# One decoder layer on one core: the first norm's outputs spread over more steps, its last squares added on VectorE, the last norm's scaled identity in one operation

## The chip, the core and the metric

The kernel runs on one core of one Trainium2 chip. The metric is the time on the device in microseconds (us), median of several runs. The engines are TensorE (PE in the profile: matrix products), VectorE (DVE), ScalarE (ACT), GpSimd (POOL) and SyncE (SP, which here only issues DMAs). Each works through its own queue of instructions in order and waits on semaphores for the others.

## What is computed

One layer of a hybrid decoder, 1024 tokens by 2048 channels, float32. What touches the change is the end of it, the output projection and the layer norm:

```python
def layer_norm(x, gain, bias):
    xf = x.astype(jnp.float32)
    mu = jnp.mean(xf, axis=-1, keepdims=True)
    var = jnp.mean(jnp.square(xf - mu), axis=-1, keepdims=True)
    y = (xf - mu) * lax.rsqrt(var + LN_EPS)
    return (y * gain.astype(jnp.float32) + bias.astype(jnp.float32)).astype(x.dtype)
...
    a = banded_sink_attention(q, k, v, sinks, bias_hqk, valid) * jax.nn.silu(g_attn)
    b = multiscale_pool(u_pool, w_pool, pool_scale) * jax.nn.silu(g_pool)
    mix = jnp.einsum('bsc,cd->bsd', jnp.concatenate([a, b], axis=-1), w_out)
    ple = jax.nn.sigmoid(jnp.einsum('bsd,de->bse', x, w_gate_ple)) * jnp.einsum('bsp,pd->bsd', p_i, w_ple)
    return layer_norm(DEEPNORM_ALPHA * x + mix + ple, ln_gain, ln_bias)
```

## The kernel before

Everything is held transposed: a tile has 128 channels on the partitions and tokens along the free dimension. The 2048 channels are 16 blocks (`NB`). Every product of a weight block with an operand is three matmuls (`mm3`, lines 181 to 183), since each float32 is split into a rounded part and a rest (`wh`, `wl` for weights, names ending in `h` and `l` for operands). The split of a weight tile `raw` is made in `make_unit`: a copy on ScalarE into `wh` (line 232) and a subtraction on VectorE into `wl` (`lo`, recorded at line 124, the helper `tt` of all two-input operations). `wh` and `wl` have four buffers each, `raw` has five of two halves, so the splits run up to four half-products ahead of TensorE. `raw` tiles are loaded on SP's queue.

The output projection runs over the last phases in two parts: the first 768 tokens (`F1`) by a seven-product scheme, and the last 256 (`F2`) plainly in `run_plain`, 16 blocks of two half-products. A half-product here is 12 matmuls of 256 columns, and every second one adds a 13th that subtracts the mean (`less_mean`, line 823). Its results lie in the PSUM banks `qa` and `qb`, two buffers each; VectorE adds each into a tile (`t1h`, `t1l`, `t2h` are parts of larger buffers that hold the 16 blocks), which is called its evacuation below. ScalarE then squares the block (line 833, into `t2l` or `t2h`), and VectorE adds the squares up.

The norm of the first 768 tokens (`one`) is finished during the plain phase of the last 256. `norm_square` has added up the squares of 15 blocks in the tile `sq`; those of the 16th stay in a tile `q` of their own. `norm_scale` sums both over the channels by matmuls with a column of ones (line 842, into `pv`), VectorE makes the variance from it (line 860), POOL raises it to the power -1/2 (`st`, through line 124), ScalarE multiplies the identity by it, block by block of 128 tokens (line 865, `dg`: six operations for 768 tokens), and a matmul with ones spreads the result over all partitions (`norm_spread`, line 849, the "spread"), which ScalarE copies back into `sq` (line 850). Then `norm_out` does, for each of the 16 blocks, a multiply on VectorE (`d` or `part` <- `sq`, 128x768), a scaling with gain and bias on ScalarE (line 127), and two DMAs to the output, on POOL's queue for the first 14 blocks and on SP's for the last two.

The norm of the last 256 tokens (`two`) comes after the last half-product and goes the same way, with two operations at line 865; its spread (line 871) stays in PSUM, and `norm_out_two` treats the blocks in pairs.

What sets the order: the kernel counts steps. One step (`tick`) is one half-product in the plain phase, 32 in all. `later(n, fn)` writes `fn` into the program n steps on. A list scheduler may then shift instructions of one engine past one another, which it did at a few places of TensorE's order.

Of the kernel before, what the change touches and what calls it, by code (L numbers as in the profile page):

```python
# [26 lines left out]
AF = mybir.ActivationFunctionType  # L27
ALU = mybir.AluOpType
# [3 lines left out]
P = 128  # L32
# [31 lines left out]
class Layer:  # L64
# [100 lines left out]
    def later(self, n, fn):  # L165

        def run():
            with ExitStack() as ctx:
                for ins in self.latest.values():
                    ctx.enter_context(self.tc.issue_after(ins))  # L170
                fn()
        self.after(n, run)
# [656 lines left out]
    def norm_square(self, L, j, d, wait=1):  # L829
        L["d"][j] = d  # L830
        last = len(L["d"]) == NB
        q = L["new"]("sq" if not L["parts"] else "q")
        self.nc.scalar.activation(q, d, AF.Square)
        if last or not L["parts"]:
            L["parts"].append(q)
        else:
            self.later(wait, lambda: self.tt(L["parts"][0], L["parts"][0], q, ALU.add))
# [14 lines left out]
    def norm_scale(self, L, wait=0):  # L852

        nc, n = self.nc, L["n"] // P
        st = self.tile(self.sm, [P, 64], "st")
        var, rstd = st[:, :n], st[:, 32 : 32 + n]
        sums = self.bank("pv", 1, (P, 16))
        for i, a in enumerate(L["parts"]):
            self.norm_sums(sums, a, i == 0, i == len(L["parts"]) - 1)
        nc.vector.tensor_scalar(out=var, in0=sums[:, :n], scalar1=1.0 / D, scalar2=EPS, op0=ALU.mult, op1=ALU.add)  # L860
        self.tt(rstd, var, self.mhalf[:, :n], ALU.pow, nc.gpsimd)
        dg = L["new"]("dg")
        for b in range(n):
            f = slice(b * P, b * P + P)
            nc.scalar.activation(dg[:, f], self.ident, AF.Copy, scale=rstd[:, b : b + 1])
        if wait:
            L["a"] = L["parts"][0]
            self.later(wait, lambda: self.norm_spread(L, L["a"], self.ones, dg))
        else:
            L["a"] = self.bank("sc", 2)[:, : L["n"]]  # L870
            nc.tensor.matmul(L["a"], self.ones, dg[:, : L["n"]], start=True, stop=True)
# [24 lines left out]
    def run(self):  # L896
        nc, tc, fix = self.nc, self.tc, self.fix
# [94 lines left out]
        parts, work, over = ExitStack(), ExitStack(), ExitStack()  # L992
# [75 lines left out]
        t = 9  # L1068
# [109 lines left out]
        for k in range(4):  # L1178
# [4 lines left out]
        one = self.one = self.norm_begin(F1, 0, lambda kind: self.tile(lns, [P, F1], "sq" if kind == "sq" else "q", F32R if kind == "hi" else F32,  # L1183
                                                                       bufs=1 if kind == "sq" else 2))
# [13 lines left out]
        for k in range(4):  # L1198
            r = rest_x[k]
            f = slice((k % 2) * 2 * F2, (k % 2) * 2 * F2 + 2 * F2)  # L1200
# [28 lines left out]

        two = self.norm_begin(F2, F1, new)  # L1230
        self.second_done = lambda b, c: self.norm_square(two, b, c)
        self.later(3, lambda: self.norm_scale(one, 1))
        for j in range(NB):
            self.later(5 + 12 * j // 16, lambda j=j: self.norm_out(one, j))
        for i in range(8):
            self.run_plain(g + i)
        self.drain()
# [58 lines left out]
```

## Time and profile before

| | |
|---|---|
| median of 3 runs | 1483.82 us |
| lowest and highest | 1481.38 and 1485.56 us |
| span of the profiled execution, first to last instruction | 1484.2 us |
| mean granted TensorE clock | 0.992 |
| plain phase, first matmul to the second norm's sums | 1412.20 to 1468.90 us |
| second norm and its outputs | 1468.90 to 1484.2 us |

The span is the only time that the profiled execution has here; nothing around it is recorded. It lies 0.4 us over the median and within the runs. Times in the profile's rows count from the start of the span. A row of the timeline shows start, length, engine, line, operation, out<-in, shape and count; in square brackets stands the idle time of the engine before it and what ended it. Lengths are from issue to completion, so the next instruction on the engine can begin before the last one's length is over.

### The profile page before, as it was taken

The page shows a single profiled execution, that of the slowest core. Times are in us where ns is not written, and L with a number is a line of the kernel's source. Part 1 is how long each engine was busy: PE and PEld are TensorE (multiplying, and loading weights), DVE is VectorE, ACT ScalarE, POOL GpSimd, SP SyncE. Part 2 cuts the span into 40 slices and gives each one's busy share as a digit, 9 for nine tenths or more (in the row PEclk, how much of TensorE's full clock was granted, in tenths as well). Part 3 has the DMA queues.
Part 4 walks back from the last instruction along what each step waited for, and adds up shares of the span by engine and source line. Part 5 has one row for each costly group of instructions (what it writes and reads, how often), then busy time and mean ns, then how long its engine had stood idle before and what let it go on. Part 6 is the DMA issues. An engine that isn't in the chain of part 4 may idle for free. (4 is left out here: it accounts for less than half of the span.)

```text
span 1484.2 us, 20552 instructions
## 1 busy us (share of the span) xinstructions
PE 1448.0 (98%) x6972; PEld 1223.3 (82%) x6972; DVE 1119.9 (75%) x2027; ACT 778.7 (52%) x1548; POOL 286.5 (19%) x404
## 2 busy tenths in 40 slices
PE   9999999999999999999999999999999999999996
PEld 6788888888887888888887778888887888899986
DVE  7788578888797877889667957675678566987785
ACT  5464566655666555666534443333256333554484
POOL 0000123332322333231111111110011111111231
PEclk9999999999999999999999999999999999999998
DMA  7563975445445555457847577987598768585464
GB/s 265 208 217 100 255 212 178 142 163 181 168 170 178 169 185 178 166 194 249 199 140 203 147 246 213 278 250 210 144 336 260 199 185 226 138 245 128 149 228 163
DMA packets 106106, 291.93 MB, mean 197 GB/s; under 512 B 12112, under 2 KB 17616, under 8 KB 106000
## 3 DMA queue, kind: packets, MB, share of 16 engines
q1 hardware_dynamic: 81936, 212.21, 42.3%
q0 software_dynamic: 20736, 71.05, 20.2%
q10 hardware_dynamic: 3328, 7.34, 1.5%
q8 instruction: 55, 0.90, 0.2%
q14 instruction: 51, 0.42, 0.1%
HBM read 200.38 MB, written 90.18 MB: 196 GB/s over the span
## 5 line engine op out<-in xcount | busy, mean ns | idle before, releaser
L232 ACT CAST wh<-raw 128x512 fp32r<-128x512 f32 x428 | 264.1, 619 | 446.0 <-PE qa L182 146.4
L124 DVE TENSOR_TENSOR wl<-raw,wh 128x512 fp32r<-128x512 f32 x428 | 299.8, 704 | 118.9 <-ACT wh L232 115.8
L402 ACT COPY part<-qa 128x512 f32<-128x512 f32 (+1 forms) x180 | 103.7, 576 | 49.7 <-PE qa L183 49.1
L607 POOL TENSOR_SCALAR_AFFINE_SELECT s<-s 128x512 fp32r<-128x512 f32 x128 | 100.6, 798 | 140.6 <-ACT s L600 99.0
L124 DVE TENSOR_TENSOR part<-part,qb 128x512 f32<-128x512 f32 (+1 forms) x120 | 80.9, 674 | 50.4 <-PE qb L183 47.7
L181 PE MATMUL qa<-b11h,wh 128*128 128x512 f32 (+2 forms) x292 | 111.1, 381 | 2.1 <-ACT b11h L258 1.4
L182 PE MATMUL qa<-b11l,wh 128*128 128x512 f32 (+2 forms) x292 | 110.0, 377 | 0.2 <-DVE b11l L124 0.2
L183 PE MATMUL qa<-b11h,wl 128*128 128x512 f32 (+2 forms) x292 | 110.0, 378 | 0.0
L181 PE MATMUL qb<-b21h,wh 128*128 128x512 f32 (+2 forms) x292 | 109.5, 375 | 0.0
L182 PE MATMUL qb<-b21l,wh 128*128 128x512 f32 (+2 forms) x292 | 108.7, 372 | 0.0
L183 PE MATMUL qb<-b21h,wl 128*128 128x512 f32 (+2 forms) x292 | 108.6, 372 | 0.0
L181 PE MATMUL qa<-t2h,wh 128*128 128x512 f32 (+1 forms) x260 | 101.5, 390 | 5.4 <-ACT part L402 3.3
L181 PE MATMUL qb<-t1h,wh 128*128 128x512 f32 (+1 forms) x260 | 100.9, 388 | 3.4 <-DVE part L124 1.4
L183 PE MATMUL qa<-t2h,wl 128*128 128x512 f32 (+1 forms) x260 | 100.8, 388 | 3.1 <-DVE wl L124 3.1
L181 PE MATMUL qa<-t3h,wh 128*128 128x512 f32 (+1 forms) x260 | 100.9, 388 | 0.2 <-ACT part L402 0.2
L181 PE MATMUL qa<-t4h,wh 128*128 128x512 f32 (+1 forms) x260 | 100.4, 386 | 0.3 <-DVE part L124 0.3
L181 PE MATMUL qb<-b22h,wh 128*128 128x512 f32 (+1 forms) x260 | 100.3, 386 | 0.0
L182 PE MATMUL qa<-t2l,wh 128*128 128x512 f32 (+1 forms) x260 | 100.1, 386 | 0.0
L182 PE MATMUL qa<-t3l,wh 128*128 128x512 f32 (+1 forms) x260 | 99.8, 384 | 0.0
L183 PE MATMUL qb<-t1h,wl 128*128 128x512 f32 (+1 forms) x260 | 99.7, 384 | 0.0
L182 PE MATMUL qb<-t1l,wh 128*128 128x512 f32 (+1 forms) x260 | 99.7, 383 | 0.0
L183 PE MATMUL qa<-t4h,wl 128*128 128x512 f32 (+1 forms) x260 | 99.7, 383 | 0.0
(288 smaller groups left out, 3562.8 us busy)
## 6 DMA issues: line engine op xcount, KB each, us to landing
raw<-in_win SPq DMA_DIRECT2D x65, 512.0 KB, 4.3
h<-part SPq DMA_DIRECT2D x34, 512.0 KB, 2.9
part<-h POOLq DMA_DIRECT2D x34, 512.0 KB, 6.7
cw<-in_wout SPq DMA_DIRECT2D x64, 256.0 KB, 3.0
raw<-in_wgate SPq DMA_DIRECT2D x32, 512.0 KB, 4.8
raw<-wc SPq DMA_DIRECT2D x32, 512.0 KB, 4.3
s<-in_x SPq DMA_DIRECT2D x44, 256.0 KB, 5.6
wc<-cw SPq DMA_DIRECT2D x32, 256.0 KB, 2.2
```

What stands on the lines that cost most here:

```text
L124: return (eng or self.nc.vector).tensor_tensor(out=out, in0=a, in1=b, op=op)
L181: mm(ps, wh, xh, start=start, stop=False, skip_group_check=True)
L182: mm(ps, wh, xl, start=False, stop=False, skip_group_check=True)
L183: return mm(ps, wl, xh, start=False, stop=stop, skip_group_check=True)
L232: self.unit_latest = [nc.scalar.copy(out=hi, in_=src).ins, L.lo(lo, src, hi).ins]
L402: self.mark("ACT", self.nc.scalar.copy(out=dst, in_=ps))
L607: nc.gpsimd.affine_select(out=o4, in_=a4, pattern=[[0, 4], [sign, P]], compare_op=ALU.is_ge, fill=0.0, base=0 if side else -1, channel_mul ...
```

## The change

It has three parts. The squares of the 16th block of the first norm are added into `sq` by VectorE like the others, and the sums are then made from one tile. The first norm's spread is written two steps after its sums instead of one, and its 16 outputs are written into steps 6 to 22 (at most one a step) instead of 5 to 16 (two in some). In the last norm the scaled identity is one VectorE multiply, in which the identity is broadcast over the token blocks and the scale along the tokens.

```diff
-        if last or not L["parts"]:
+        if not L["parts"] or (last and not L["at"] == 0):
             L["parts"].append(q)
         else:
             self.later(wait, lambda: self.tt(L["parts"][0], L["parts"][0], q, ALU.add))
...
         dg = L["new"]("dg")
-        for b in range(n):
-            f = slice(b * P, b * P + P)
-            nc.scalar.activation(dg[:, f], self.ident, AF.Copy, scale=rstd[:, b : b + 1])
+        if wait:
+            for b in range(n):
+                f = slice(b * P, b * P + P)
+                nc.scalar.activation(dg[:, f], self.ident, AF.Copy, scale=rstd[:, b : b + 1])
+        else:
+            each = [t.broadcast_to([P, n, P]) for t in (self.ident.rearrange("p (b t) -> p b t", b=1), rstd.rearrange("p (b t) -> p b t", t=1))]
+            self.tt(dg[:, : n * P].rearrange("p (b t) -> p b t", b=n), *each, ALU.mult)
...
-        self.later(3, lambda: self.norm_scale(one, 1))
+        self.later(3, lambda: self.norm_scale(one, 2))
         for j in range(NB):
-            self.later(5 + 12 * j // 16, lambda j=j: self.norm_out(one, j))
+            self.later(6 + 18 * j // 16, lambda j=j: self.norm_out(one, j))
```

TensorE's order around the first norm's spread, before; `qb_13404` and `qa_13472` are the results of two half-products that follow each other:

```order
L183 MATMUL qb_13404<-b21h_13335,wl_13368 128x256
L823 MATMUL qb_13404<-two_12350,w_2357_12156 128x256
L181 MATMUL qa_13472<-b11h_13334,wh_13385 128x256
L182 MATMUL qa_13472<-b11l_13336,wh_13385 128x256
L849 MATMUL sc_13465<-q_13439,ones 128x512
L849 MATMUL sc_13468<-q_13439,ones 128x256
L183 MATMUL qa_13472<-b11h_13334,wl_13386 128x256
```

The same place now; `qa_13461` is what was `qa_13472`:

```order
L182 MATMUL qa_13461<-b11l_13337,wh_13386 128x256
L183 MATMUL qa_13461<-b11h_13335,wl_13387 128x256
L849 MATMUL sc_13480<-q_13434,ones 128x512
L849 MATMUL sc_13483<-q_13434,ones 128x256
L181 MATMUL qa_13461<-b21h_13336,wh_13406 128x256
```

The spread has moved from behind the second matmul of that half-product to behind its twelfth.

VectorE's order in the middle of the first norm's outputs, before; the 128x768 rows are the outputs' multiplies, the 128x256 rows with `qa` or `qb` evacuations, those of `t2l` additions of squares:

```order
L124 TENSOR_TENSOR wl_13623<-raw_13383,wh_13622 128x512
L124 TENSOR_TENSOR part_12461<-part_12461,sq_12501 128x768
L124 TENSOR_TENSOR part_12462<-part_12462,sq_12501 128x768
L124 TENSOR_TENSOR wl_13649<-raw_13421,wh_13648 128x512
L124 TENSOR_TENSOR t1l_13347<-t1l_13347,qb_13621 128x256
L124 TENSOR_TENSOR part_12614<-part_12614,sq_12501 128x768
L124 TENSOR_TENSOR wl_13674<-raw_13421,wh_13673 128x512
```

The same blocks now:

```order
L124 TENSOR_TENSOR wl_13696<-raw_13478,wh_13695 128x512
L124 TENSOR_TENSOR part_12461<-part_12461,sq_12501 128x768
L124 TENSOR_TENSOR t2l_13366<-t2l_13366,t2h_13349 128x256
L124 TENSOR_TENSOR wl_13718<-raw_13527,wh_13717 128x512
L124 TENSOR_TENSOR t1l_13348<-t1l_13348,qb_13694 128x256
L124 TENSOR_TENSOR part_12462<-part_12462,sq_12501 128x768
L124 TENSOR_TENSOR wl_13743<-raw_13527,wh_13742 128x512
```

The two multiplies that stood in a row now have a split, an evacuation and an addition between them.

## The prediction, made before the result was known

> **What bounds the kernel now.** I read the page first. TensorE is busy 98% of the span and every slice up to the last shows 9, so a change to the last two phases can only pay where TensorE stands still.
>
> ```profile
> span 1484.2 us, 20552 instructions
> PE 1448.0 (98%) x6972; PEld 1223.3 (82%) x6972; DVE 1119.9 (75%) x2027; ACT 778.7 (52%) x1548; POOL 286.5 (19%) x404
> ```
>
> Then I cut the last phase (the 256 tokens, lines 471 to 489) into stretches. The columns are busy microseconds of PE, PEld, DVE, ACT, POOL, the granted clock, the DMA share and GB/s.
>
> ```profile
> 1412.20:1424.20 12.00, 10.43 (x82) 9.70 (x82) 6.21 (x13) 6.84 (x16) 1.75 (x1) 1.00 0.30 92
> 1424.20:1437.60 13.40, 13.40 (x116) 13.20 (x114) 13.34 (x22) 12.83 (x21) 7.11 (x13) 1.00 0.75 254
> 1437.60:1451.00 13.40, 11.17 (x82) 10.05 (x83) 13.40 (x23) 12.90 (x19) 8.12 (x15) 1.00 0.94 334
> 1451.00:1469.10 18.10, 18.10 (x157) 18.10 (x155) 12.10 (x25) 8.33 (x16) 0.00 (x0) 1.00 0.39 148
> 1469.10:1484.20 15.10, 1.61 (x9) 1.04 (x8) 6.19 (x12) 6.29 (x13) 3.04 (x5) 0.63 0.42 139
> ```
>
> While the first norm's outputs run (1424 to 1451) VectorE is full, and in the second half of that TensorE is not: VectorE sets the pace there. After 1451 TensorE never waits. The last 15 us are a serial tail. The waits of TensorE in this phase, and the TensorE rows around the first norm's sums, are these (start, length, engine, line, operation):
>
> ```profile
> PE sc L849 <- ACT q L865: 1.6, 1, 1.6
> PE qb L181 <- ACT wh L232: 0.8, 2, 0.4
> PE qb L183 <- DVE wl L124: 0.6, 1, 0.6
> PE qa L183 <- DVE wl L124: 0.4, 1, 0.4
> PE qa L181 <- ACT wh L232: 0.4, 1, 0.4
> ...
> 1416.56 1.39 PE L842 MATMUL pv<-ones,sq 128*128 128x1 f32 x12
> 1417.81 1.48 PE L842 MATMUL pv<-ones,q 128*128 128x1 f32 x12
> 1419.15 0.36 PE L181 MATMUL qb<-b21h,wh 128*128 128x256 f32 x1
> ...
> 1420.60 0.28 PE L823 MATMUL qb<-two,w 128*128 128x256 f32 x1
> ...
> 1420.84 0.28 PE L182 MATMUL qa<-b11l,wh 128*128 128x256 f32 x1
> 1422.69 1.56 PE L849 MATMUL sc<-q,ones 128*128 128x512 f32 x4 [1.57 <-ACT q L865]
> 1423.89 0.47 PE L183 MATMUL qa<-b11h,wl 128*128 128x256 f32 x1
> 1426.71 0.28 PE L181 MATMUL qb<-b11h,wh 128*128 128x256 f32 x1
> 1429.65 0.28 PE L181 MATMUL qa<-b11h,wh 128*128 128x256 f32 x1
> ...
> 1468.90 0.50 PE L842 MATMUL pv<-ones,t2l 128*128 128x1 f32 x4
> ```
>
> From 1426.71 to 1429.65 stand 25 matmuls, so one is 0.1176 us and the phase's 400 are 47.04. From 1412.20 to the second norm's sums at 1468.90 it takes 56.70. Off that go 2.59 for the sums (1416.56 to 1419.15), 1.20 for the spread (1422.69 to 1423.89) and 1.73 for the wait ahead of it (1420.84 plus 0.12, to 1422.69). 4.14 us are left: the other waits listed and the slow first matmul behind each.
>
> **Part 1, the last squares.** Six of the twelve sum matmuls go: 1417.81 to 1419.15, 1.34 us. In their place VectorE adds one 128x768 tile, and the sums wait for it. Is it ready in time?
>
> ```profile
> 1414.22 0.84 ACT L833 ACTIVATE q<-d 128x768 f32<-128x768 f32 x1
> ...
> 1414.45 1.28 DVE L124 TENSOR_TENSOR wl<-raw,wh 128x512 fp32r<-128x512 f32 x2
> ...
> 1437.46 1.82 DVE L124 TENSOR_TENSOR part<-part,sq 128x768 f32<-128x768 f32 x2
> 1439.20 0.69 DVE L124 TENSOR_TENSOR wl<-raw,wh 128x512 fp32r<-128x512 f32 x1
> 1439.80 0.41 DVE L124 TENSOR_TENSOR t1l<-t1l,qb 128x256 f32<-128x256 f32 x1
> 1440.13 0.95 DVE L124 TENSOR_TENSOR part<-part,sq 128x768 f32<-128x768 f32 x1
> ```
>
> The squares end at 1415.06. The add stands behind the first of the two wl and takes 0.87 (two 128x768 rows run from 1437.46 to 1439.20), so it ends at about 1415.95, 0.6 before TensorE gets to the sums at 1416.56. Behind it in VectorE's queue are one wl, the first evacuation and another wl, each 0.87 later; the delayed wl is wanted at 1419.3 and is there by 1416.6. Cost nothing; with the cover gone, at most 0.87.
>
> **Part 2, the wait before the spread.** The order now puts the spread ten matmuls later. With the sums done at 1417.81 the power, and the scaled identity on ScalarE, come 1.34 earlier.
>
> ```profile
> 1419.58 1.75 POOL L124 TENSOR_TENSOR st<-st,mhalf 128x6 f32<-128x6 f32 x1 [13.40 <-DVE st L860]
> 1421.36 1.86 ACT L865 ACTIVATE q<-ident,st 128x128 f32<-128x128 f32 x6 [4.11 <-POOL st L124]
> 1420.92 0.42 DVE L124 TENSOR_TENSOR t1h<-t1h,qb 128x256 f32<-128x256 f32 x1 [0.82 <-PE qb L823]
> ```
>
> ScalarE begins at 1421.36 - 1.34 = 1420.02 and the spread can start 1.33 behind that (1422.69 - 1421.36), at 1421.35. TensorE gets there 25 matmuls after 1417.81, at 1420.75. The wait is 0.60 instead of 1.73: 1.13 saved. The spread ends at 1422.55. The first multiply of the outputs now stands behind the evacuation of the half-product that follows: its 13th matmul starts at 1423.96, the evacuation 0.32 later (1420.60 to 1420.92), and 0.33 for it (1439.80 to 1440.13) brings the multiply to 1424.61.
>
> **Part 3, the outputs over 17 steps.** No work is removed: 16 multiplies on VectorE, 16 scalings on ScalarE, and 28 DMAs on POOL's queue and 4 on SP's stay, with no two multiplies in a row (SP now issues the last two weight tiles ahead of its four). What counts is how VectorE's queue then runs against TensorE. Its pitches from the rows above: 0.87 a multiply, 0.60 a wl (1439.20 to 1439.80), 0.33 an evacuation or an addition of squares. Before, from the first multiply to wl_13747, the last wl that TensorE waited for, the order has 15 multiplies, 11 wl and 10 short rows.
>
> ```profile
> 1424.82 1.83 DVE L124 TENSOR_TENSOR d<-d,sq 128x768 f32<-128x768 f32 x2
> ...
> 1447.28 0.68 DVE L124 TENSOR_TENSOR wl<-raw,wh 128x512 fp32r<-128x512 f32 x1
> ...
> 1448.02 0.38 PE L183 MATMUL qb<-b11h,wl 128*128 128x256 f32 x1
> ```
>
> That is 13.05 + 6.60 + 3.30 = 22.95, and 1424.82 + 22.95 = 1447.77, where the trace has 1447.28 + 0.60 = 1447.88: the queue ran without a gap. TensorE goes on at 1448.02, 0.25 behind my sum, with 171 matmuls to go, 20.11 us; it needs 20.88, so one more wait for a wh and its restart cost 0.77.
>
> In the new order the last such wl is wl_13857: 15 multiplies, 16 wl and 15 short rows, 13.05 + 9.60 + 4.95 = 27.60. From 1424.61 with the same 0.25: 1452.46. From there TensorE has 96 matmuls, 11.29, and again wants a wh too early (0.77): 1464.52 instead of 1468.90. That is 4.38 us, of which 1.34 are the sums and 1.13 the wait, and 1.9 come from the later waits, which shrink from 4.14 to about 2.2 and do not vanish.
>
> The queue's pitch is what this rests on. The Trainium skill (VectorE: DVE Perf Modes, The DRAIN you can't avoid) says that after each operation "the next op does not start until the 8-stage pipe empties", and that one which isn't held starts earlier. By its first half each row would cost its full length, 0.95, 0.68 and 0.42, the two chains would differ by 5.5 us and not 4.65, and the gain would be 3.5; the rows start 0.08 before the last one ends, so I keep the pitches.
>
> **Part 4, the tail.** Two ScalarE operations become one VectorE multiply with both inputs broadcast.
>
> ```profile
> 1470.98 0.72 POOL L124 TENSOR_TENSOR st<-st,mhalf 128x2 f32<-128x2 f32 x1 [20.75 <-DVE st L860]
> 1471.73 0.69 ACT L865 ACTIVATE t2l<-ident,st 128x128 f32<-128x128 f32 x2 [1.69 <-POOL st L124]
> 1472.47 0.70 PE L871 MATMUL sc<-t2l,ones 128*128 128x256 f32 x2 [1.78 <-ACT t2l L865]
> ...
> L124 DVE TENSOR_TENSOR cw<-cw,wmean x32: 670/686/1140, 390.4 to 668.3; 128x512 f32<-128x512 f32 x32
> ```
>
> All of this is on the path, nothing hides it. The cw row is line 789, whose second input is broadcast along the innermost dimension too; at 0.686 for 512 elements it costs what the wl of that size does (0.68). So 256 elements cost the 0.42 of the row at 1420.92, and 0.69 - 0.42 = 0.27 is saved. Bounds: 0.69 saved if it were free, 0.45 lost at cw's worst (1.14). I take 0.27.
>
> **Sum.** 4.38 + 0.27 = 4.65, against the span of 1484.2; the median of the three runs, 1483.82, is 0.4 under it, and I take the gain off the median: 1479.2. A measurement of this kernel tells about 0.3%, 4.45 us, from no change, so the forecast lies on that line.
>
> **Rivals.** *VectorE gets gaps.* Its queue is in order, and seven evacuations stand in the new chain ahead of wl rows. Before, it ran so late that no evacuation found TensorE unfinished. It now runs about 3 us less late at the end; if each of the seven waits 0.33, the chain is 2.3 longer, and the time is 1481.5. Against it: TensorE still ends up waiting for wl in my sum, so the evacuations should find finished banks.
>
> *No later wait is left.* If VectorE's lead holds, TensorE runs 1412.20 + 47.04 + 1.25 (the six sums left) + 1.20 + 0.60 = 1462.29, and with the tail the gain is 6.88: 1476.9. For it, the average need a step falls; against it, VectorE's need over the 17 steps (16 multiplies, 17 wl and 17 short rows, 29.7) is still above TensorE's 17 times 12.5 matmuls, 25.0.
>
> *Slower: weight tiles come late.* The output DMAs now run on until the last weight tiles load.
>
> ```profile
> raw<-wc SPq DMA_DIRECT2D x15, 512.0 KB, 5.8
> ...
> SPq L138 <- DVE wl L124: 64.4, 12, 25.5
> ```
>
> There are five buffers: a load starts when VectorE has split the tile five ahead of it, which leaves it four tiles of 2.94 us of TensorE, 11.8 us, against 5.8 to land. It costs something only from 11.8 on, and turns the result only from 20.9 (11.8 + 4.65 + 4.45); there the time is 1488.3. Against it, the queue waits for VectorE and not for bytes, and the same output bytes are spread over more time.
>
> That the change doesn't do what it says is excluded: the order shows six sum matmuls gone, the moved multiplies and the single operation in the tail.
>
> **How the numbers follow.** The forecast 0.60, gaps 0.23, no wait left 0.13, late weights 0.04. Of the forecast's 0.60, 0.35 lies beyond 4.45 us. Faster: 0.35 + 0.13 = 0.48; the same: 0.25 + 0.23 = 0.48; slower: 0.04. The range goes from the second rival (1476.9, less the 0.4 by which the tail may gain more) to the first (1481.5, plus the 0.7 by which the tail may cost more): 1476.5 to 1482.2; the forecast's own is 1477.9 to 1480.6.
>
> **What would show it.** One group of twelve L842 records (six matmuls) where there were two, and the next matmul at about 1417.8; a wait of about 0.6 before the spread; VectorE without a gap from about 1424.6 to 1454; waits for wl of 0.3 at most between 1440 and 1453 and two for wh; the second norm's sums at 1464.5; one VectorE row of 0.42 ahead of L875, and from the power's end to that matmul 0.5 instead of 0.77. I am wrong if VectorE shows waits on evacuations in that stretch, if TensorE waits at the first sums, or if the tail from the second norm's sums to the end is not shorter.

## The result: 0.9962 of the time before, and the profile after

| | before | after |
|---|---|---|
| median of 8 runs each | 1484.99 us | 1478.22 us |
| lowest and highest | 1481.38 and 1489.01 us | 1476.12 and 1480.79 us |
| ratio, with its 95% interval | | 0.9962, 0.9949 to 0.9975 |
| ratio of the repetition (e4) | | 0.9951, 0.9940 to 0.9963 |
| span of the profiled execution | 1484.2 us | 1474.6 us |
| last phase, first matmul to the second norm's sums | 56.70 us | 52.53 us |
| tail, from there to the end | 15.30 us | 14.97 us |

Against the 1484.99 the ratio is 5.6 us, with 3.7 to 7.6 as its interval; the two medians by themselves lie 6.8 us apart. The two profiled spans lie 9.6 us apart, but 5.1 of that arise ahead of the change: the last phase begins at 1407.10 instead of 1412.20, after instructions that are the same in both kernels. What the change can have done is in the last two rows: 4.17 + 0.33 = 4.50 us.

The stretches of the last phase, after (columns as in the prediction):

```profile
1407.10:1418.00 10.90, 10.51 (x83) 9.78 (x83) 7.38 (x14) 6.99 (x16) 1.74 (x1) 1.00 0.32 103
1418.00:1432.40 14.40, 14.40 (x125) 14.40 (x124) 13.95 (x25) 13.36 (x23) 6.36 (x12) 1.00 0.76 252
1432.40:1446.00 13.60, 13.12 (x106) 12.35 (x104) 13.60 (x25) 12.63 (x21) 7.20 (x14) 1.00 0.97 354
1446.00:1459.60 13.60, 13.18 (x109) 12.98 (x110) 10.22 (x21) 7.65 (x13) 1.66 (x4) 1.00 0.41 154
1459.60:1474.60 15.00, 1.84 (x12) 1.27 (x10) 6.61 (x13) 5.59 (x11) 3.03 (x5) 0.67 0.42 140
```

VectorE is still all but full from 1418 to 1446 (13.95 of 14.40 us, then 13.60 of 13.60), but TensorE, which was busy for 11.17 of 13.40 us in the second of these stretches before, is now busy for 13.12 of 13.60. TensorE's waits in the phase and the tail, and its rows at the first norm's sums and at the two waits for a `wh`:

```profile
PE sc L875 <- DVE t2l L124: 1.5, 1, 1.5
PE pv L842 <- ACT t2l L833: 0.7, 1, 0.7
PE qb L181 <- ACT wh L232: 0.4, 1, 0.4
PE qa L181 <- ACT wh L232: 0.4, 1, 0.4
PE sc L849 <- ACT q L866: 0.4, 1, 0.4
...
1411.46 1.39 PE L842 MATMUL pv<-ones,sq 128*128 128x1 f32 x12
1412.71 0.36 PE L181 MATMUL qb<-b21h,wh 128*128 128x256 f32 x1
...
1415.58 0.28 PE L183 MATMUL qa<-b11h,wl 128*128 128x256 f32 x1
1416.25 1.56 PE L849 MATMUL sc<-q,ones 128*128 128x512 f32 x4 [0.39 <-ACT q L866]
1417.45 0.47 PE L181 MATMUL qa<-b21h,wh 128*128 128x256 f32 x1
...
1446.02 0.39 PE L181 MATMUL qb<-b11h,wh 128*128 128x256 f32 x1 [0.41 <-ACT wh L232]
1449.64 0.39 PE L181 MATMUL qa<-b11h,wh 128*128 128x256 f32 x1 [0.40 <-ACT wh L232]
```

One group of sums takes 1.25 us (1411.46 to 1412.71) where two took 2.59. The wait ahead of the spread is 0.55 (1415.58 plus 0.12, to 1416.25) where it was 1.73. The waits for a `wl` are no longer in the list. VectorE, and the tail:

```profile
1410.00 0.96 DVE L124 TENSOR_TENSOR sq<-sq,q 128x768 f32<-128x768 f32 x1
...
1419.37 0.42 DVE L124 TENSOR_TENSOR t1l<-t1l,qa 128x256 f32<-128x256 f32 x1 [0.45 <-PE qa L823]
1419.71 0.95 DVE L124 TENSOR_TENSOR d<-d,sq 128x768 f32<-128x768 f32 x1
...
1447.76 0.95 DVE L124 TENSOR_TENSOR d<-d,sq 128x768 f32<-128x768 f32 x1
...
1461.70 0.72 POOL L124 TENSOR_TENSOR st<-st,mhalf 128x2 f32<-128x2 f32 x1 [13.25 <-DVE st L860]
1462.45 0.43 DVE L124 TENSOR_TENSOR t2l<-ident,st 128x256 f32<-128x256 f32 x1 [0.84 <-POOL st L124]
1462.93 0.70 PE L875 MATMUL sc<-t2l,ones 128*128 128x256 f32 x2 [1.51 <-DVE t2l L124]
```

The added addition starts at 1410.00, its successor 0.87 later, and its row ends at 1410.96, 0.5 before TensorE's sums. From the first multiply at 1419.71 to the sixteenth at 1447.76 no row of VectorE has an idle time in brackets.

### The profile page after: what moved, and what is told of

Same layout as the page of the kernel before. It is cut to its first block, busy times and chain, and to the rows that moved or that the text cites. A ratio compares the mean times of both kernels' runs of the same rounds, so it can differ in the third digit from the quotient of the medians.

```text
span 1474.6 us, 20528 instructions
## 1 busy us (share of the span) xinstructions
PE 1445.2 (98%) x6960; PEld 1222.0 (83%) x6960; DVE 1119.8 (76%) x2029; ACT 777.8 (53%) x1546; POOL 287.9 (20%) x404
## 5 line engine op out<-in xcount | busy, mean ns | idle before, releaser
L182 PE MATMUL qb<-b22l,wh 128*128 128x512 f32 (+1 forms) x260 | 99.7, 384 | 0.0
```

The source lines that it names most:

```text
L182: mm(ps, wh, xl, start=False, stop=False, skip_group_check=True)
```

## The experiments

All were timed against the kernel before on the same chip. "Phase" is from the first matmul of the last phase to the second norm's sums, "tail" from there to the end, "wait" the gap ahead of the spread, "later waits" all later gaps of TensorE in the phase with the slow first matmuls behind them; each comes from the one profiled execution of its kernel, by the start times of the matmuls. The clock column is the granted clock behind the first norm's sums.

| kernel | sum matmuls | clock | phase | wait | later waits | tail | ratio (95%) |
|---|---|---|---|---|---|---|---|
| before | 12 | 1.00 | 56.70 | 1.73 | 4.00 | 15.30 | |
| after | 6 | 1.00 | 52.53 | 0.55 | 2.25 | 14.97 | 0.9962 (0.9949 to 0.9975) |
| e0 before again | 12 | fell | 58.68 | 1.12 | 5.14 | 15.60 | 1.0006 (0.9995 to 1.0017) |
| e1 squares | 6 | 1.00 | 55.29 | 1.02 | 4.64 | 15.80 | 0.9989 (0.9976 to 1.0001) |
| e2 later and wider | 12 | fell | 54.71 | 0 | 2.19 | 15.30 | 0.9981 (0.9972 to 0.9991) |
| e3 tail | 12 | 1.00 | 56.76 | 1.68 | 3.94 | 15.19 | 0.9991 (0.9977 to 1.0005) |
| e4 after again | 6 | 1.00 | 52.52 | 0.56 | 2.29 | 15.54 | 0.9951 (0.9940 to 0.9963) |
| e5 later | 12 | fell | 57.07 | 0.09 | 4.69 | 15.77 | 0.9990 (0.9978 to 1.0003) |
| e6 wider | 12 | fell | 54.54 | 0.41 | 1.54 | 15.85 | 0.9978 (0.9967 to 0.9989) |
| e7 widest | 6 | 1.00 | 50.39 | 0.55 | 0 | 15.03 | 0.9954 (0.9942 to 0.9966) |
| e8 short multiplies | 12 | fell | 57.39 | 0.96 | 3.60 | 15.26 | one run |
| e9 short scalings | 12 | 1.00 | 56.79 | 1.73 | 4.13 | 15.23 | one run |
| e10 three times the sums | 18 | fell | 57.68 | 0.10 | 2.29 | 14.96 | one run |
| e11 widest and later | 6 | 1.00 | 49.64 | 0 | 0 | 15.04 | 0.9949 (0.9929 to 0.9969) |

**e0: the kernel before, again.** No edit.

> The kernel before, unchanged, profiled a second time. In the first profiles the last phase began at 1412.2 us before and at 1407.1 us after, 5.1 us apart, although the instructions ahead of it are the same. Theory (scatter of the executions): this second profile begins the phase anywhere from 1406 to 1414, and the phase itself again takes 56.7 us and the tail 15.3, both within 0.2; the time is within 0.15% of before. Rival (something ahead of the phase differs between the two kernels, the place of code or data): the phase begins at 1412 again, within 1 us.

The phase began at 1408.92, 3.3 us ahead of the first profile of the same instructions: the start scatters by itself, and is not the same within 1 us as the rival had it. The phase was not 56.7 us as both expected but 58.68. The granted clock says why; the stretches are from the first sum matmul on, 3.4 us each:

```profile
1413.20:1416.60 3.40, 3.40 (x33) 3.40 (x32) 0.82 (x3) 0.65 (x2) 0.39 (x1) 1.00 0.78 259
1416.80:1420.20 3.40, 2.58 (x10) 1.90 (x9) 0.43 (x2) 2.21 (x8) 1.16 (x1) 0.50 0.02 8
1420.20:1423.60 3.40, 3.40 (x12) 2.57 (x11) 2.00 (x4) 1.45 (x3) 0.00 (x0) 0.50 0.34 96
1424.00:1427.40 3.40, 3.40 (x31) 3.40 (x31) 2.83 (x5) 3.33 (x6) 1.34 (x3) 1.00 0.10 40
```

The third number from the right is TensorE's clock: 1.00, then 0.50 for 6.8 us, then 1.00. The phase became 1.98 us longer; the rest of what the slow clock costs lies in the wait for the spread, which shrank from 1.73 to 1.12. Of the later waits of 5.14, about 1.1 are steps at the slow clock (up to 1423.71); the rest, about 4.0, is as before. The tail, 15.60, missed the 15.3 expected; e3 says why.

**e1: the squares alone.**

```diff
-        if last or not L["parts"]:
+        if not L["parts"] or (last and not L["at"] == 0):
```

> Only the last squares are added by VectorE. Theory: six sum matmuls go (1.34 us) and everything behind them moves up by as much, since VectorE's first multiply does too: phase 55.4 us (before 56.7), wait ahead of the spread unchanged at 1.7, tail 15.3; time ratio 0.999. Rival (VectorE's extra add makes the sums wait): a gap of 0.3 to 0.9 us at the first sums, and a phase of 55.9 to 56.3.

The phase is 55.29, 1.41 under before, as expected. The sums start 4.36 us into the phase in both kernels (1412.41 to 1416.77, and 1412.20 to 1416.56), so they did not wait for the addition and the rival is out. The wait was expected to stay at 1.7 and is 1.02, with later waits of 4.64 instead of 4.00: in this trace the spread stands eight matmuls into the half-product and not two, so TensorE reaches it later, and what the wait lost the later ones took up. The two together are 5.66, before 5.73. The tail, 15.80 where 15.3 was expected, is explained under e3.

**e2: the numbers of steps alone.**

```diff
-        self.later(3, lambda: self.norm_scale(one, 1))
+        self.later(3, lambda: self.norm_scale(one, 2))
...
-            self.later(5 + 12 * j // 16, lambda j=j: self.norm_out(one, j))
+            self.later(6 + 18 * j // 16, lambda j=j: self.norm_out(one, j))
```

> Only the two numbers of steps are changed (spread two steps after the sums, outputs in steps 6 to 22). Theory: wait ahead of the spread 0.6 us (before 1.7), later waits of TensorE together about 2.2 (before 4.1): phase 53.7 us, tail 15.3; ratio 0.998. Rival (the gain of the whole change is mostly that of the sums, and the later waits only move): phase 55.5 us or more.

Later waits of 2.19, as expected, against 4.00. The phase is 54.71 and not 53.7, since the clock fell here too, for 3.4 us:

```profile
1410.50:1413.90 3.40, 3.40 (x32) 3.40 (x32) 0.74 (x3) 0.63 (x2) 0.33 (x1) 1.00 0.81 287
1414.10:1417.50 3.40, 3.40 (x18) 3.40 (x18) 0.42 (x1) 2.15 (x8) 1.21 (x1) 0.50 0.00 0
1417.60:1421.00 3.40, 3.40 (x24) 2.87 (x24) 2.00 (x4) 2.33 (x5) 0.00 (x0) 1.00 0.33 110
```

The rival, that the waits only move, is out.

**e3: the tail alone.** The edit is that of `norm_scale` in the change.

> Only the last norm's scaled identity is one VectorE operation. Theory: phase 56.7 us as before, tail 15.0 (before 15.3); from the end of the power to the spread of the last norm 0.5 us instead of 0.77; ratio 0.9998, not to be told from 1. Rival (the two broadcast inputs make the operation slow): the operation takes 0.7 us or more and the tail is 15.3 or longer.

The operation takes 0.43 us (the row of the changed kernel at 1462.45 is the same), so the rival is out, and from the power's end to the spread it is 0.51, as expected; the whole tail, 15.19, is only 0.11 shorter than that of before. The tails of all kernels with the old form lie between 15.23 and 15.85, with the new one between 14.96 and 15.54: they scatter by more than the step is worth.

The traces show where the scatter comes from. From the power's start to the spread it is 1.49 or 1.50 us in all eight profiles with the old form and 1.23 in all six with the new one, and from the spread's end to the end of the span 10.98 to 11.00 us in all fourteen. What differs is the spread itself, two matmuls. They take 0.70 us where the clock fell to 0.50 behind them (1472.47 before, 1462.93 after) and up to 1.22 where it fell ahead of them, as in e1 and in e4:

```profile
1471.27 1.22 PE L871 MATMUL sc<-t2l,ones 128*128 128x256 f32 x2 [1.78 <-ACT t2l L865]
...
1461.57 1.22 PE L875 MATMUL sc<-t2l,ones 128*128 128x256 f32 x2 [1.51 <-DVE t2l L124]
```

Among the profiles with the spread at the full clock, the old form (before, e2, e8, e9) has tails of 15.23 to 15.30 and the new one (after, e7, e10, e11) of 14.96 to 15.04: the step is worth 0.26 in every trace.

**e4: the changed kernel, again.** No edit.

> The changed kernel, unchanged, profiled a second time. Theory: phase 52.5 us and tail 15.0 again, each within 0.2 unless the granted clock falls in it; the place where the phase begins differs from 1407.1, since it only scatters. In the profiles so far the granted clock fell to 0.5 some 3.5 us after the first norm's sums in two of four kernels with twelve sum matmuls (2 us lost and 1.0 us lost) and in none of two with six; by the theory that the shorter stretch of one-column matmuls keeps the clock up, it stays at 1.00 here too. Rival (the clock falls at random there): it falls here as well, and the phase is 53.5 to 55. Time ratio 0.996 to 0.997.

Phase 52.52, clock 1.00, as expected. The tail is 15.54 and not 15.0: this is the profile above in which the clock fell ahead of the last spread. The time ratio, 0.9951, is better than the 0.996 to 0.997 expected; the interval reaches into it.

**e5 and e6: later alone, and wider alone.** e5 puts the spread and the outputs one step later and keeps 12 steps; e6 spreads the outputs over 17 steps and moves nothing else.

```diff
 # e5
-        self.later(3, lambda: self.norm_scale(one, 1))
+        self.later(3, lambda: self.norm_scale(one, 2))
...
-            self.later(5 + 12 * j // 16, lambda j=j: self.norm_out(one, j))
+            self.later(6 + 12 * j // 16, lambda j=j: self.norm_out(one, j))
 # e6
-            self.later(5 + 12 * j // 16, lambda j=j: self.norm_out(one, j))
+            self.later(5 + 18 * j // 16, lambda j=j: self.norm_out(one, j))
```

> Only the spread one step later and the outputs one step later, still over 12 steps (6 to 17); twelve sum matmuls. Theory: the wait ahead of the spread falls from 1.7 to 0.6, but VectorE has as much to do in as few steps, so the later waits stay at 4 or rise to 4.5: phase 56.1 us at a full clock, ratio 0.9996. Rival (the two waits are one thing, and later is enough): later waits of 2.5 or less, phase 54 us.

> Only the outputs over 17 steps instead of 12 (5 to 21); the spread where it was; twelve sum matmuls. Theory: wait ahead of the spread 1.7 as before, later waits 1.6 to 2.2 instead of 4.0: phase 54.5 us at a full clock, ratio 0.9985. Rival (the later waits only move behind the outputs): later waits of 3.5 or more, phase 56.2 or more.

The later waits are 4.69 in e5 (4 to 4.5 expected, 2.5 or less by the rival) and 1.54 in e6 (1.6 to 2.2 expected, 3.5 or more by the rival). Both lie just outside their ranges, but on the theory's side: the later waits follow the number of steps. The clock fell behind the sums in both, which took up most of the wait ahead of the spread (0.09 and 0.41) and adds some to the phase: 57.07 against 56.1 expected in e5, and 54.54 in e6, where 56.70 less 2.46 of later waits would be 54.24.

**e7: the changed kernel with the outputs over 22 steps.**

```diff
-            self.later(6 + 18 * j // 16, lambda j=j: self.norm_out(one, j))
+            self.later(6 + 23 * j // 16, lambda j=j: self.norm_out(one, j))
```

> The changed kernel with the outputs over 22 steps (6 to 27) instead of 17. Theory: over 22 steps VectorE needs 22 times 0.93 and 16 times 0.87, 34.4 us, against 32.3 of TensorE, an excess of 2.1 that its lead of four half-products covers, so the later waits all but vanish (under 0.5): phase 50.6 us, tail 15.0, ratio 0.995. Rival (the last outputs now come too late and hold up the second norm's additions or the output DMAs): the tail grows past 15.5 or TensorE waits in the last five steps.

```profile
1420.00:1433.00 13.00, 13.00 (x112) 13.00 (x111) 12.55 (x22) 11.83 (x20) 4.83 (x9) 1.00 0.70 222
1433.00:1446.00 13.00, 13.00 (x113) 13.00 (x112) 13.00 (x24) 12.01 (x20) 6.10 (x12) 1.00 0.97 350
1446.00:1459.70 13.70, 13.70 (x119) 13.70 (x118) 12.26 (x23) 10.35 (x17) 4.35 (x8) 1.00 0.61 226
```

TensorE is busy throughout, the later waits are gone and the phase is 50.39, 2.1 under the changed kernel; the tail (15.03) does not suffer. The runs don't show it: 0.9954 with an interval that overlaps that of e4 almost wholly.

**e8 and e9: is it VectorE or ScalarE?** In the kernel before, the multiplies (e8) or the scalings (e9) of the first norm's outputs are done on 256 of 768 columns.

```diff
 # e8
-        self.tt(d, d, L["a"], ALU.mult)
+        self.tt(d[:, :F2], d[:, :F2], L["a"][:, :F2], ALU.mult)
 # e9
-        self.ident_act(d, d, self.c(C_B + j), self.c(C_G + j))
+        self.ident_act(d[:, :F2], d[:, :F2], self.c(C_B + j), self.c(C_G + j))
```

> The kernel before, with each of the sixteen multiplies of the first norm's outputs done on 256 of its 768 columns (the other columns of these outputs are left unscaled), so VectorE has 16 times 0.54 us less to do in the same 12 steps; ScalarE's scalings stay whole. Theory of the prediction (VectorE alone sets TensorE's pace there): VectorE's need falls under TensorE's, and the later waits from 4.0 us to 1 or less. Rival (ScalarE is next: 12.8 to 12.9 of 13.4 us busy in the same two stretches): later waits of 2 to 3.

> The kernel before, with each of the sixteen scalings on ScalarE done on 256 of its 768 columns (the other columns get no gain and bias), so ScalarE has 16 times 0.5 us less or somewhat under; VectorE's multiplies stay whole. Theory: VectorE still sets the pace, later waits of 3.5 to 4.2 as before (4.0). Rival (ScalarE sets the pace): later waits of 2 or less.

The busiest 13.5 us of e8, then of e9:

```profile
1438.00:1451.50 13.50, 12.34 (x95) 11.29 (x94) 10.22 (x24) 13.50 (x21) 8.89 (x17) 1.00 0.99 360
...
1433.00:1446.50 13.50, 11.21 (x84) 9.87 (x83) 13.50 (x23) 9.35 (x18) 7.09 (x14) 1.00 0.97 350
```

With short scalings nothing changes: VectorE is full (13.50), ScalarE is not (9.35), later waits 4.13. With short multiplies VectorE falls to 10.22, but ScalarE is full, 13.50. Of e8's 3.60, 0.92 are steps of the slow clock (up to 1428.95 in its trace); the later waits proper are 2.68, and not 1 or less. So VectorE does set the pace before, and ScalarE is right behind it: taking work from VectorE alone would have brought 1.3 us.

**e10: the sums three times over.**

```diff
-        for i, a in enumerate(L["parts"]):
+        parts = L["parts"] * (3 if wait else 1)
+        for i, a in enumerate(parts):
```

> The changed kernel with the six sum matmuls of the first norm done three times over (eighteen; the variance comes out three times too large), so the stretch of one-column matmuls is 3.8 us instead of 1.25. The granted clock fell after the sums in four of six profiles with twelve of them and in none of four with six. Theory (the length of that stretch makes the clock fall): it falls to 0.5 some 3 to 5 us behind the first sum, for 3.4 us or longer, and the phase takes 56 to 57.5 us. Rival (it falls at random): clock 1.00, phase 55.0 (52.5 and 12 times 0.21).

```profile
1410.92 4.38 PE L842 MATMUL pv<-ones,sq 128*128 128x1 f32 x36
...
1413.00:1414.00 1.00, 1.00 (x11) 1.00 (x11) 0.00 (x0) 0.00 (x0) 0.00 (x0) 1.00 0.78 221
1414.00:1415.00 1.00, 1.00 (x9) 1.00 (x9) 0.00 (x0) 0.00 (x0) 0.00 (x0) 0.76 0.62 254
1415.00:1416.00 1.00, 1.00 (x6) 1.00 (x6) 0.67 (x2) 0.00 (x0) 0.41 (x1) 0.50 0.05 20
...
1421.00:1422.00 1.00, 1.00 (x3) 0.34 (x2) 0.64 (x1) 0.33 (x1) 0.00 (x0) 0.82 0.39 74
```

The clock fell 3.6 us behind the first sum, for 6.8 us, and the phase is 57.68, a little over the 56 to 57.5 expected and 2.7 over the 55.0 that the extra matmuls alone would make.

**e11: widest, and the spread one step later still.**

```diff
-        self.later(3, lambda: self.norm_scale(one, 2))
+        self.later(3, lambda: self.norm_scale(one, 3))
...
-            self.later(6 + 18 * j // 16, lambda j=j: self.norm_out(one, j))
+            self.later(7 + 23 * j // 16, lambda j=j: self.norm_out(one, j))
```

> The changed kernel with the spread one step later still (three behind the sums) and the outputs over 22 steps (7 to 28). Theory: no wait ahead of the spread (0.55 in the changed kernel) and no later waits: phase 49.8 to 49.9 us, tail 15.0 to 15.8 as the clock goes; ratio to the kernel before 0.9945 to 0.995. Rival (the times of the runs don't follow the phase any more, since the clock's falls elsewhere decide): ratio 0.9955 to 0.9965 in spite of a phase of 49.9.

Phase 49.64, no wait anywhere in it: 2.9 us under the changed kernel by the trace. The ratio, 0.9949, is the best of all, but its interval (0.9929 to 0.9969) covers those of e4 and e7, so the runs don't show that it beats the changed kernel; against before they do.

## Why the prediction was right, point by point

*The squares* (1.34 us forecast): 1.34 measured in the sums' rows, 1.41 in the phase when done alone (e1). The addition's row ended 0.5 before the sums, where 0.6 was worked out.

*The wait ahead of the spread* (1.73 to 0.60 forecast): 0.55 and 0.56 in the two profiles of the changed kernel.

*The later waits* (4.14 to about 2.2 forecast; two for a `wh`, those for a `wl` at most 0.3): counted as the prediction counted them, as all that is left of the phase, they are 2.49 (52.53 less 47.04, 1.25, 1.20 and 0.55), and by the gaps alone they went from 4.00 to 2.25. So they shrank by 1.65 to 1.75 and not by 1.9. There are two of 0.57 for a `wh` and none over 0.21 for a `wl`; with the slow matmul behind each, the two for a `wh`, which ScalarE makes, are 1.3 of the 2.25. e5 and e6 tie them to the number of steps, e9 to VectorE. The two chains, with the pitches of 0.87, 0.60 and 0.33, hold: the first multiply came 0.20 later than forecast (12.61 us into the phase instead of 12.41, because the first matmul behind the spread again took 0.31 and not 0.12), and so did the second norm's sums (52.53 into it instead of 52.32).

*The tail* (0.27 forecast): from the power's start to the spread 1.23 instead of 1.49, so 0.26; the operation took 0.43 and not the 0.42 of the row. The tail as a whole also depends on the clock at the last spread, which the prediction did not have: in e4 it is 15.54, so not shorter than the 15.30 of before, which the prediction had named as a sign of being wrong. The step itself is as long there as in the first profile (1.23).

*The rivals.* Gaps in VectorE's chain: there are none. No later wait left: not here; it is what e7 reaches with five steps more. Late weight tiles: TensorE nowhere waits for one in the phase, though the DMA engines are busy 97% of the time from 1432 to 1446.

*The time.* The forecast was 1479.2 us and the median 1478.2, but that this came within 1.0 us is in part luck. The forecast was taken off the median of three runs, 1483.8, and that of eight is 1485.0; off that median the forecast gain of 4.65 would have given 1480.3, 2.1 us over the measured one.

*What it did not have.* The sum of 4.65 is 4.50 in the one trace (and 3.94 in e4, with its longer tail), but the runs gained 5.6 and, in the repetition, 7.3 us (0.0049 of 1483.3). One thing that lies between was not in the prediction: the clock behind the first norm's sums. It fell in five of the eight profiles with twelve sum matmuls and in none of the five with six. The traces leave chance little room: it fell behind the sums in exactly those profiles in which 2.05 us or more of them lay in one window of 3.413 us, and stayed up where at most 1.96 us did (shown in the last section; the limit was read off afterwards; ahead of their runs e4 had been forecast to stay up and e10 to fall, and both did). The change leaves 1.25 us of sums, which is under that limit wherever the window lies. With twelve, 2.59 us of sums, 2.0 or more fall into one window in 0.59 of all positions (0.82 and twice 0.59, of 3.41), an estimate that takes every position as equally likely.

In the kernel before a fall cost 2.0 us (e0); in e2 and e6, which have other waits, it cost about 0.8 (54.71 against 52.53 + 1.34) and 0.3 (see there). Six tenths of one of these is some 0.2 to 1.2 us, an estimate, which brings 4.5 to between 4.7 and 5.7: inside the first interval (3.7 to 7.6), and just into that of the repetition (5.5 to 8.9) at its upper end. When the clock falls is shown; how much of the gain in the runs this makes is only estimated.

*What stays open.* The start of the phase lay anywhere from 1405.74 (e4) to 1414.45 (e8) with the same instructions ahead of it. In e4 the clock never fell before the phase; in the first profile of before and in e8 it fell near 10, 465 and 880 us. Others don't fit as well (e5, with all three, began at 1409.96), and no run was made on it.

## What to carry to other kernels

Work that runs beside a matmul phase costs nothing as long as each helper engine's need for a step, operands and extras together, stays under the phase's step or is covered by the operands' lead: count both over the steps the extras are spread over, and spread the extras until they fit (here 22 steps were enough and 12 and 17 were not; none between was run). Count the second-busiest engine too, since taking work from the first only moves the limit to it. And a row of tiny matmuls in the middle of a dense phase costs more than its own length if the granted clock falls behind it; here half the row kept it up in all five profiles.

## What the runs showed of the hardware

The granted clock falls without TensorE ever standing still for long: in e0 the first sum starts at 1413.19, the clock is 0.50 from about 1416.8, and in between TensorE had one-column matmuls for 2.6 us and otherwise dense 256-column ones, with no gap over 0.2. It came back after 3.41 us (e2, e5, e6) or 6.83 us (e0, e8, e10).

In each of the thirteen traces with more than one change of the clock, all changes lie whole multiples of 3.4133 us apart, to 0.001 us, so the windows can be counted back from a later change to the first norm's sums. What tells the profiles apart is how much of the sums lies in one window:

| profile | sums | most of them in one window | clock at its end |
|---|---|---|---|
| after, e1, e4, e7, e11 | 1.25 or 1.26 us | 1.25 or 1.26 us | 1.00 |
| e3 | 2.60 us | 1.46 us | 1.00 |
| before | 2.59 us | 1.89 us | 1.00 |
| e9 | 2.59 us | 1.96 us | 1.00 |
| e5 | 2.59 us | 2.05 us | 0.50 |
| e6, e0, e2, e8 | 2.88, 2.60, 2.59, 2.59 us | 2.30, 2.38, 2.44, 2.59 us | 0.50 |
| e10 | 4.24 us | 3.41 us | 0.50 |

The sums are taken from the first one's start to the start of the next 256-column matmul; those of e6 and e10 ran on into the slow clock.

The two that lie closest to the limit, by their windows: e9, where the clock stays, and e5, where it falls.

```profile
1410.69:1414.10 3.41, 3.41 (x33) 3.41 (x31) 1.56 (x4) 1.66 (x3) 0.00 (x0) 1.00 0.57 174
1414.10:1417.51 3.41, 2.60 (x22) 2.40 (x22) 1.19 (x3) 0.57 (x2) 1.74 (x1) 1.00 0.34 138
...
1414.86:1418.28 3.42, 3.42 (x32) 3.42 (x32) 0.77 (x2) 0.16 (x1) 0.94 (x1) 1.00 0.70 231
1418.28:1421.69 3.41, 3.41 (x17) 3.26 (x16) 0.79 (x2) 2.57 (x8) 0.80 (x1) 0.50 0.00 1
```

In both the profile has TensorE busy for the whole window that holds most of the sums, so the clock does not go by that busy time: the one-column matmuls, which are busy there, lower what it goes by.

The Trainium skill (TensorE: Matmul & The Clock Gate, Part 1: The HAM clock gate) describes a free-running window of 3413 ns at whose end the clock is halved or restored by how busy TensorE was; the lengths and the 0.50 agree with it. The Trainium skill's table on the same page, in the section Why this matters for your kernels, asks for no idle gaps over about 3 us. That was kept here, with no gap over 0.2 us in e0's window, and the clock fell all the same.

A slow clock costs less where TensorE would have waited anyway, since the matmuls at half the clock use up the wait ahead of the spread. In e2 and e5 it is 0 and 0.09 us, and 0.55 at the full clock in the changed kernel, where the spread has the same place; in e6 it is 0.41, and 1.73 before.

A VectorE multiply with both inputs broadcast, one along the innermost dimension, took 0.43 us for 128x256; the other rows of that size shown here take 0.41 and 0.42.
